# A decoder layer on one core: FFN2's norm takes its second columns by squares and an exchange, with three blocks summed meanwhile

## The chip, the cores and the metric

The kernel runs on one core of one Trainium2 chip. The metric is the device time of the whole program in microseconds, the median of several runs. A core has a matrix engine (TensorE, here PE), three engines for elementwise work (VectorE: DVE, ScalarE: ACT, GpSimd: POOL) and a queue engine, SyncE (SP), which issues most of the transfers between main memory and the on-chip memory. Matmul results land in PSUM, eight banks of 128 rows by 512 float32 columns.

## The reference

One layer on 256 tokens of 1024 columns, all float32. Both feed-forward parts (FFN1 and FFN2) have 2816 hidden columns.

```python
h = x
h = h + 0.5 * swiglu(rms_norm(h, ffn1_norm), ffn1_w_gate, ffn1_w_up, ffn1_w_down)
h = h + hybrid_mixer(rms_norm(h, mix_norm), ...)      # projection, two attentions, gates, W_out
h = h + 0.5 * swiglu(rms_norm(h, ffn2_norm), ffn2_w_gate, ffn2_w_up, ffn2_w_down)
out = rms_norm(h, final_norm)

swiglu(x, g, u, d) = (silu(x @ g) * (x @ u)) @ d
rms_norm(x, g) = x * rsqrt(mean(x * x) + 1e-6) * g
```

## The kernel before

The 256 tokens are two halves of 128, t = 0 and t = 1. Every weight matrix is cut into tiles of 128 x 512, which lie in main memory as one stream `wstream`, in the order of use; a DMA on SP fetches a chunk of two tiles (512 KB) into a buffer `raw`. The first 12 chunks have buffers of their own, all later ones share three, so that a chunk's DMA starts when DVE has read the second tile of the chunk three before it. Each tile is split into a high part `wh` by ACT (L163 and L160) and the rest `wl` by DVE (L164 and L161), in ten buffers each. Activations are split likewise (`zh` and `zl` for the norm "z" ahead of FFN2). A product is three matmuls, wh with the high activations, wl with the high ones, and wh with the low ones (`mm3`, L292 to L294). These three are called a unit here. A split buffer comes free when t = 1 has used its tile.

FFN1 and FFN2 each run through 11 blocks of 256 hidden columns. A block is eight tiles k = 0 to 7 (128 rows of the model dimension each, gate and up side by side) for each t, and its sums fill one PSUM bank for each t. `hidden(b, t)` then evacuates a bank: ACT takes the silu of its first 256 columns (L432), DVE multiplies it with the other 256 (L433) and transposes the product in blocks of 32 x 32 (L441). Within a block t = 1 lags t = 0 by some units (`lagged`): by 2 from block 1 on, by 8 in FFN2's block 0. FFN1's block 0 goes by pairs (`unit_pair`).

PSUM comes in three kinds: `acc_bank` (one bank, 3 buffers), `y_bank` (one, 1 buffer) and `two_banks` (one tile of two banks, 2 buffers). FFN1's block 0 takes one two-bank tile for both t, later blocks take `acc_bank`.

The order of PE and SP is written by hand; the other engines' order is too, except in stretches where a scheduler places their instructions. `Weave` lets side work advance by a step with each unit (`tick`), after a delay given in units (the constants `D_...`). `W.pump` splits weight tiles ahead.

A norm's activations need the tokens' rows transposed (`Normed`). The first 512 columns (c = 0) go by `moved`: DVE transposes squares of 32 x 32, 16 DMAs exchange the squares, and ACT and DVE split the result. The second 512 columns (c = 1) go by `half`: four PE transposes (`tp_z`, 128 x 128 each) into PSUM, then the split. The factor 1/rms (`inv_rms`) is applied in `hidden`. At the start x comes in transposed from the host already (`xt`), and x itself (`h`, two loads of 512 KB) is needed only for the squares of the norm and for the residual.

Of the kernel before, what the change touches and what calls it, by code (L numbers as in the profile page):

```python
# [8 lines left out]
F32 = mybir.dt.float32  # L9
# [12 lines left out]
KD = D // P  # L22
# [22 lines left out]
D_NORM = 4  # L45
D_SQUARES = 3
D_EIGHT = 6
D_MERGE = 8
D_FIRST = (9, 10)
D_RMS0 = 4  # L50
D_RMS1 = 5
AHEAD0 = 4
N_WARM = 10
D_LANE = 11
# [134 lines left out]
def hybrid_layer_kernel(ctx, tc, x, xt, pos, g_final, bgate, wstream, out):  # L189
    nc = tc.nc  # L190
# [18 lines left out]
    def big(nm, dt=F32R):  # L209
        return work.tile([P, 1024], dt, name=nm, tag="big", bufs=24)  # L210
# [16 lines left out]
    def gain(i):  # L227
        for n, (lo, hi) in enumerate(((0, FB * KD), (W_IN, W_BR), (W_FFN2, W_FFN2 + FB * KD))):
            if lo <= i < hi:
                k = n * KD + (i - lo) % KD  # L230
                return gk[:, k:k + 1]
        return None

    W = Weights(nc, wpool, lambda nm: big(nm, F32), wstream, gain, WB, AHEAD0)
# [17 lines left out]
    load_x(nc.sync, 6, 8)  # L252
    W.load(4)
    nc.sync.dma_start(h[0], x[0:P, :])
    W.load(5)
    nc.sync.dma_start(h[1], x[P:T, :])
    W.load(6)
    nc.sync.dma_start(posi, pos)


# [35 lines left out]
    def unit(o, a, w, first, last):  # L296
        mm3(o, a[0], a[1], w, first, last)
        weave.tick()
        W.pump()
# [12 lines left out]
    def split(dst_h, dst_l, src, hi_engine=None, rest=nc.vector):  # L312
        (hi_engine or nc.scalar.copy)(dst_h, src)
        rest.tensor_sub(dst_l, src, dst_h.bitcast(F32))
# [26 lines left out]
    class Normed:  # L341
# [15 lines left out]
        def moved(self, c):  # L357
# [7 lines left out]
            split(plain(self.parts[0][:, s]), plain(self.parts[1][:, s]), slots(q[:, 512:1024], 4))  # L365
            self.there.add(c)

        def rms(self):
            weave.begin(inv_rms(self.t, self.nm, self.r))

# [4 lines left out]
    class Given(Normed):  # L375
# [15 lines left out]
        def blk(self, k):  # L391
            o = k % 4 * T + self.t * P
            return [q[:, o:o + P] for q in self.made[k // 4 * 2:k // 4 * 2 + 2]]

    def lagged(n, lag):

        for k in range(n + lag):
            if k < n:
                yield 0, k
            if k >= lag:  # L400
                yield 1, k - lag
# [4 lines left out]
    def slots(q, n):  # L406

        return q[:, 0:n * P].rearrange("p (g s w) -> p s g w", g=4, s=n)

    def plain(q):  # L410
        return q.rearrange("p (s g w) -> p s g w", g=4, w=32)

    def exchange(moved, squares, n, queues, gap):

        w = 32
        for m in range(16):
            i, j = divmod(m, 4)
            queues[m % len(queues)].dma_start(moved[j * w:j * w + w, i * n * w:(i + 1) * n * w],
                                              squares[i * w:i * w + w, j * n * w:(j + 1) * n * w])
            if m % len(queues) == len(queues) - 1:  # L420
                yield gap


    def ffn(base, xn, nm, on_half, lag, last=False):


        hts = {}
        squares = {}

        def hidden(b, t, bank):  # L430
            sh = wide(f"sh_{nm}{b}_{t}", 512)
            silu = nc.scalar.activation(sh[:, 0:256], bank[:, 0:256], AF.Silu, scale=xn[t].r)  # L432
            prod = nc.vector.scalar_tensor_tensor(sh[:, 256:512], bank[:, 256:512], xn[t].r, sh[:, 0:256],  # L433
                                                  op0=ALU.mult, op1=ALU.mult)
            marks["silu"], marks["prod"] = silu.ins, prod.ins
            p = b // 2
            n = min(8, 4 * (FB - 2 * p))
            if p not in squares:
                squares[p] = big(f"hs_{nm}{b}", F32)
            dst = slots(squares[p], n)[:, b % 2 * 4 + t:b % 2 * 4 + t + 3:2]  # L440
            nc.vector.transpose(dst, plain(sh[:, 256:512]))  # L441
            if t == 1 and (b % 2 or b == FB - 1):
                weave.add(turn_hidden(p, n), D_TURNED)

        def later(f, *args):
            f(*args)
            return
            yield

        def turn_hidden(p, n):  # L450
            moved = big(f"hm_{nm}{p}", F32)
            yield from exchange(moved, squares[p], n, [nc.sync], D_MOVE)
            yield D_MOVED
            hts[p] = big(f"hth_{nm}{p}"), big(f"htl_{nm}{p}")
            split(plain(hts[p][0][:, 0:n * P]), plain(hts[p][1][:, 0:n * P]), slots(moved, n))

        for b in range(FB):
            if b == 1:
                W.ahead = AHEAD
            if b == 1 and last:  # L460
                ordered.enter_context(tc.manual_schedule())
            banks = {}
            if b == 0 and lag == 0:
                pair = two_banks(f"gu_{nm}0")
                banks = {t: pair[:, t * 512:t * 512 + 512] for t in range(2)}
                for k in range(KD):
                    unit_pair([banks[t] for t in range(2)], [xn[t].blk(k) for t in range(2)], W.get(base + k),
                              k == 0, k == KD - 1)
                    W.done(base + k)
                for t in range(2):  # L470
                    weave.add(later(hidden, b, t, banks[t]), D_FIRST[t])
            for t, k in lagged(KD, 2 if b else lag) if b or lag else ():
                if k == 0:
                    banks[t] = acc_bank(f"gu_{nm}{b}_{t}")
                i = base + b * KD + k
                unit(banks[t], xn[t].blk(k), W.get(i), k == 0, k == KD - 1)
                if t == 1:
                    W.done(i)
                if k == KD - 1:
                    weave.add(later(hidden, b, t, banks[t]), 0 if b else D_FIRST[t])  # L480

        base += FB * KD
        banks = {}

        def out_bank(t, c):
            if (t, c) not in banks:
                if (t, c) != (1, 1):
                    banks[t, c] = acc_bank(f"dn_{nm}{t}{c}")
                else:
                    banks[t, c] = y_bank(f"dn_{nm}{t}{c}")  # L490
            return banks[t, c]

        def down(t, c, k, i, piece=None):

            o = k % 4 * 256 + t * P
            ht = [q[:, o:o + P] for q in hts[k // 4]]
            w = W.get(i)
            if piece is not None:
                if k == head:
                    banks[piece] = two_banks(f"dn_{nm}p{piece}")  # L500
                cols = slice(piece * 256, piece * 256 + 256)
                mm3(banks[piece][:, 0:256], *ht, [q[:, cols] for q in w], k == head, k == KF - 1)
                weave.tick()
                W.pump()
            else:
                unit(out_bank(t, c), ht, w, k == 0, k == (head - 1 if last and (t, c) == (1, 1) else KF - 1))

        def residual(t, c, piece=None):
            if piece is None:
                ps, s = banks[t, c][:, 0:512], slice(c * 512, c * 512 + 512)  # L510
            else:
                ps = banks[piece][:, 0:256]
                s = slice(c * 512 + piece * 256, c * 512 + piece * 256 + 256)
            nc.vector.scalar_tensor_tensor(h[t][:, s], ps, 0.5, h[t][:, s], op0=ALU.mult, op1=ALU.add)

        tail = TAILS[2 if last else 1]
        head = KF - tail
        for k in range(head):
            for c in range(2):
                for t in range(2):  # L520
                    down(t, c, k, base + 2 * k + c)
                W.done(base + 2 * k + c)
        if not last:
            ordered.close()
        weave.flush()
        if last:

            residual(1, 1)
        for t, c in ((0, 0), (0, 1), (1, 0), (1, 1)) if last else ((0, 0), (1, 0), (0, 1), (1, 1)):
            pieces = (0, 1) if last and (t, c) == (1, 1) else (None,)  # L530
            for piece in pieces:
                for k in range(head, KF):
                    i = base + 2 * head + c * tail + k - head
                    down(t, c, k, i, piece)
                    if t == 1 and piece in (None, 1):
                        W.done(i)
                residual(t, c, piece)
                on_half(t, c, piece)
# [84 lines left out]
    un = [None, None]  # L623

    def next_norm(dst, nm):
        def on_half(t, c, piece=None):
            def go():
                dst[t].half(c)
                dst[t].rms()
                return  # L630
                yield

            if c == 0:
                dst[t] = Normed(t, nm)
                weave.begin(dst[t].moved(c))
            else:
                weave.add(go(), D_NORM)

        return on_half
# [415 lines left out]
```

## Time and profile before

| what | value |
|---|---|
| median of 3 runs | 556.6 us (556.47 to 556.66) |
| the profiled execution | 555.9 us, its span 554.2 us |
| busy PE | 546.1 us (99%) |
| busy DVE, ACT, POOL | 401.3 us (72%), 338.1 us (61%), 70.1 us (13%) |
| mean granted TensorE clock | 0.997 |
| read from main memory | 102.25 MB |

The span goes from the first to the last instruction. What the time holds beyond it (555.9 - 554.2 = 1.7 us) is not in the trace. Busy shares are means over all stages. Where PE is named with a wait, nothing else hid it. One matmul's own duration is printed as 0.39 us, but matmuls are pipelined: the distance from one to the next is what counts.

### The profile page before, as it was taken

The numbers are of one execution on the slowest core, as the hardware profiler recorded it, in microseconds if no ns is written. First come the engines' busy times: TensorE is split into PE (matmuls) and PEld (weight loads), VectorE is DVE, ScalarE is ACT, GpSimd is POOL, SyncE is SP. The second block draws the span as 40 slices with busy tenths as digits, with TensorE's granted clock in tenths as the row PEclk, the third lists the DMA queues.
The fourth block names the chain that finished last, engine by engine and source line by source line (L and its number), as shares of the span: only waits on it lengthen the run. The fifth ranks groups of instructions, "written<-read, shape, count | busy, mean of one in ns | idle before, by whom it ended". The sixth has DMA issues, their size and how long they took to land.

```text
span 554.2 us, 7853 instructions
## 1 busy us (share of the span) xinstructions
PE 546.1 (99%) x2494; PEld 449.5 (81%) x2494; DVE 401.3 (72%) x694; ACT 338.1 (61%) x576; POOL 70.1 (13%) x141
## 2 busy tenths in 40 slices
PE   9999999999999999999999999999999999999995
PEld 5788888888888888888888888888888888888884
DVE  6887788766466676889888888777677678655645
ACT  6865656655454767677875774476556566544633
POOL 1200000000003746022022200460000000000000
PEclk9999999999999999999999999999999999999998
DMA  8946766775685677455545464576657766757722
GB/s 311 403 141 202 220 216 216 220 237 184 210 235 179 200 232 220 155 159 183 176 151 172 137 202 149 179 242 216 219 180 234 238 206 200 229 179 230 243 79 76
DMA packets 42937, 111.69 MB, mean 202 GB/s; under 512 B 8080, under 2 KB 16528, under 8 KB 42896
## 3 DMA queue, kind: packets, MB, share of 16 engines
q1 hardware_dynamic: 40464, 107.90, 60.9%
q0 software_dynamic: 2000, 2.62, 1.8%
q10 hardware_dynamic: 432, 0.67, 0.3%
q8 instruction: 19, 0.31, 0.3%
q14 instruction: 22, 0.18, 0.1%
HBM read 102.25 MB, written 1.05 MB: 186 GB/s over the span
## 4 chain that ended last, share of the span: by engine, by line
PE 95%; DMA 3%; ACT 0%; DVE 0%; issue 0%; ACTq 0%
PE gu_f L293 14%; PE gu_f L294 14%; PE gu_f L292 14%; PE dn_f L294 7%; PE dn_f L292 7%; PE dn_f L293 7%; PE in L292 7%; PE in L294 7%; PE in L293 7%; DMA raw<-in_wstream 2%; PE wo L294 1%; PE wo L292 1%; PE wo L293 1%; PE y_a L748 1%; PE z L748 1%; PE y_b L748 1%
## 5 line engine op out<-in xcount | busy, mean ns | idle before, releaser
L164 DVE SCALAR_TENSOR_TENSOR wl<-raw,first,wh 128x512 fp32r<-128x512 f32 x256 | 181.8, 747 | 41.3 <-ACT wh L163 40.1
L163 ACT ACTIVATE wh<-raw,first 128x512 fp32r<-128x512 f32 x256 | 171.7, 717 | 56.3 <-DMA raw<-in_wstream 31.0
L160 ACT CAST wh<-raw 128x512 fp32r<-128x512 f32 x120 | 70.4, 620 | 63.9 <-DMA raw<-in_wstream 40.8
L161 DVE TENSOR_TENSOR wl<-raw,wh 128x512 fp32r<-128x512 f32 x120 | 78.6, 691 | 40.0 <-ACT wh L160 39.9
L292 PE MATMUL gu_f<-wh,zh 128*128 128x512 f32 x176 | 68.6, 390 | 0.0
L294 PE MATMUL gu_f<-wh,zl 128*128 128x512 f32 x176 | 68.5, 389 | 0.0
L293 PE MATMUL gu_f<-wl,zh 128*128 128x512 f32 x176 | 68.5, 389 | 0.0
L292 PE MATMUL dn_f<-wh,hth_f 128*128 128x512 f32 x172 | 67.1, 390 | 0.0
L294 PE MATMUL dn_f<-wh,htl_f 128*128 128x512 f32 x172 | 66.9, 389 | 0.0
L293 PE MATMUL dn_f<-wl,hth_f 128*128 128x512 f32 x172 | 66.9, 389 | 0.0
L292 PE MATMUL in<-wh,uh 128*128 128x512 f32 x160 | 63.5, 397 | 0.0
L293 PE MATMUL gu_f<-wl,xh 128*128 128x512 f32 x160 | 62.4, 390 | 0.3 <-DVE wl L164 0.3
L294 PE MATMUL in<-wh,ul 128*128 128x512 f32 x160 | 62.5, 391 | 0.0
L292 PE MATMUL gu_f<-wh,xh 128*128 128x512 f32 x160 | 62.4, 390 | 0.1
L293 PE MATMUL in<-wl,uh 128*128 128x512 f32 x160 | 62.4, 390 | 0.0
L294 PE MATMUL gu_f<-wh,xl 128*128 128x512 f32 x160 | 62.2, 389 | 0.0
L293 PEld LDWEIGHTS gu_f<-wl,zh 128*128 128x128 f32 x176 | 33.0, 188 | 6.9
L294 PEld LDWEIGHTS gu_f<-wh,zl 128*128 128x128 f32 x176 | 33.0, 188 | 6.8
L292 PEld LDWEIGHTS gu_f<-wh,zh 128*128 128x128 f32 x176 | 33.0, 188 | 6.8
L292 PEld LDWEIGHTS dn_f<-wh,hth_f 128*128 128x128 f32 x172 | 32.3, 188 | 6.9 <-DVE sh_f L433 0.4
L294 PEld LDWEIGHTS dn_f<-wh,htl_f 128*128 128x128 f32 x172 | 32.3, 188 | 6.7
L293 PEld LDWEIGHTS dn_f<-wl,hth_f 128*128 128x128 f32 x172 | 32.3, 188 | 6.7
(247 smaller groups left out, 756.5 us busy)
## 6 DMA issues: line engine op xcount, KB each, us to landing
raw<-in_wstream SPq DMA_DIRECT2D x184, 512.0 KB, 4.3
hm_f<-hs_f SPq DMA_DIRECT2D x160, 32.0 KB, 4.2
raw<-in_wstream SPq DMA_DIRECT2D x8, 256.0 KB, 4.9
h<-in_x SPq DMA_DIRECT2D x2, 512.0 KB, 6.6
bg<-in_bgate POOLq DMA_DIRECT2D x4, 256.0 KB, 4.6
xin<-in_xt SPq DMA_DIRECT2D x3, 256.0 KB, 5.1
hm_f<-hs_f SPq DMA_DIRECT2D x32, 16.0 KB, 3.1
gB<-in_g_final POOLq DMA_DIRECT2D x1, 512.0 KB, 6.2
```

The costliest lines, as they stand in the source:

```text
L160: self.nc.scalar.copy(hi, raw)
L161: self.nc.vector.tensor_sub(lo, raw, hi.bitcast(F32))
L163: self.nc.scalar.activation(hi, raw, AF.Copy, scale=g)
L164: self.nc.vector.scalar_tensor_tensor(lo, raw, g, hi.bitcast(F32), op0=ALU.mult, op1=ALU.subtract)
L292: nc.tensor.matmul(o, ah, wh, start=first, stop=False)
L293: nc.tensor.matmul(o, ah, wl, start=False, stop=False)
L294: nc.tensor.matmul(o, al, wh, start=False, stop=last)
L748: nc.tensor.matmul(o, a[p], b[q], start=first and i == 0, stop=last and i == 2, skip_group_check=True)
```

## The change

Three things are moved.

At the start, the DMA of the second half of x is issued after weight chunk 5 (tiles 10 and 11) and no longer before it. The square of that half (`D_RMS1`) and FFN1's `hidden(0, 1)` (`D_GIVEN`) come later by some units.

In the norm ahead of FFN2, the second columns of both t no longer take PE's transposes. `moved_both` transposes squares on DVE for t = 0 and then t = 1, exchanges both together by 16 DMAs of 32 KB on SP and POOL, and splits the result.

So that FFN2 can begin without the second columns, `three_blocks` sums the blocks 0, 1 and 2 on the first columns first (24 units with a lag of 8), and then on the second columns (24 units with a lag of 2). The weight stream's order on the host follows, and so does `gain`. Six sums are open meanwhile: blocks 0 and 1 of one t take the two halves of one two-bank tile (`gu_f2 01`), block 2 takes an `acc_bank`. The order is written by hand from block 3 on, where it was from block 1 on.

```diff
-D_FIRST = (9, 10)
+D_GIVEN = (9, 15)
-D_RMS1 = 5
+D_RMS1 = 9
...
     nc.sync.dma_start(h[0], x[0:P, :])
-    W.load(5)
+    W.load(6)
     nc.sync.dma_start(h[1], x[P:T, :])
-    W.load(6)
     nc.sync.dma_start(posi, pos)
...
+        @staticmethod
+        def moved_both(c, norms):
+
+            s = slice(c * 512, c * 512 + 512)
+            squares, moved = [big(f"{norms[0].nm}{i}{c}", F32) for i in "sm"]
+            for t in range(2):
+                nc.vector.transpose(slots(squares, 8)[:, t:t + 7:2], plain(h[t][:, s]))
+                yield None if t == 0 else D_SQUARES
+            yield from exchange(moved, squares, 8, [nc.sync, nc.gpsimd], 1)
+            yield D_BOTH
+            for t in range(2):
+                split(plain(norms[t].parts[0][:, s]), plain(norms[t].parts[1][:, s]), slots(moved, 8)[:, t:t + 7:2])
+                norms[t].there.add(c)
+                yield 1
...
+    def three_blocks(x, base, banks, evac):
+
+        for c in range(2):
+            for t, n in lagged(12, 2 if c else KD):
+                b, k = divmod(n, 4)
+                i = base + c * 12 + n
+                unit(banks(t, b), x[t].blk(c * 4 + k), W.get(i), c == 0 and k == 0, c == 1 and k == 3)
+                if t == 1:
+                    W.done(i)
+                if c == 1 and k == 3:
+                    evac(b, t, banks(t, b))
...
-            if b == 1 and last:
+            if b == 3 and last:
                 ordered.enter_context(tc.manual_schedule())
...
+            if b == 0 and lag:
+                gus = {}
+
+                def gu_bank(t, b):
+                    if (t, b) not in gus:
+                        if b == 0:
+                            pair = two_banks(f"gu_{nm}01{t}")
+                            gus[t, 0], gus[t, 1] = pair[:, 0:512], pair[:, 512:1024]
+                        else:
+                            gus[t, b] = acc_bank(f"gu_{nm}{b}_{t}")
+                    return gus[t, b]
+
+                three_blocks(xn, base, gu_bank, lambda b, t, ps: weave.add(later(hidden, b, t, ps)))
+            for t, k in lagged(KD, 2) if b > (2 if lag else 0) else ():
...
+            elif nm == "z":
+                weave.add(later(dst[t].rms), D_NORM)
+                if t == 0:
+                    both.append(Normed.moved_both(c, dst))
+                    next(both[0])
+                else:
+                    weave.begin(both[0])
...
+        if n == 2:
+            res = [res[b * KD + c * 4 + k] for c in range(2) for b in range(3) for k in range(4)] + res[3 * KD:]
```

Three places show how instructions move. The first is PE in FFN2, where block 0 ends and the next sum goes on. `wh251` is the high part of tile 251; `gu_f20_0` is block 0 of t = 0 and `gu_f20_1` block 0 of t = 1. Before, block 0 of t = 1 ends and block 1 begins in another bank, waiting for its weights alone (`waits DVE` on a row with a `wl` is for that part):

```order
L292 MATMUL gu_f20_1_4035<-wh251_3982,zh1_3829 128x512
L293 MATMUL gu_f20_1_4035<-wl251_3983,zh1_3829 128x512
L294 MATMUL gu_f20_1_4035<-wh251_3982,zl1_3830 128x512
L292 MATMUL gu_f21_0_4082<-wh252_3991,zh0_3766 128x512 [waits Activation_49]
L293 MATMUL gu_f21_0_4082<-wl252_3992,zh0_3766 128x512 [waits DVE_49]
L294 MATMUL gu_f21_0_4082<-wh252_3991,zl0_3767 128x512
```

In the change, `gu_f2010` is the two-bank tile of blocks 0 and 1 for t = 0, and `gu_f2011` that for t = 1. The tiles 256 to 259 are block 0 on the second columns, and 260 is block 1's first tile there:

```order
L294 MATMUL gu_f2010_3966<-wh259_4102,zh0_3766 128x512
L295 MATMUL gu_f2010_3966<-wl259_4103,zh0_3766 128x512
L296 MATMUL gu_f2010_3966<-wh259_4102,zl0_3767 128x512
L294 MATMUL gu_f2011_4043<-wh257_4084,zh1_3829 128x512
L295 MATMUL gu_f2011_4043<-wl257_4085,zh1_3829 128x512
L296 MATMUL gu_f2011_4043<-wh257_4084,zl1_3830 128x512
L294 MATMUL gu_f2010_3966<-wh260_4113,zh0_3766 128x512 [waits DVE_49]
L295 MATMUL gu_f2010_3966<-wl260_4114,zh0_3766 128x512
L296 MATMUL gu_f2010_3966<-wh260_4113,zl0_3767 128x512
```

Block 0 of t = 0 is complete with tile 259, one unit of t = 1 follows, and then tile 260 adds to block 1 of t = 0 in the same two-bank tile, with a wait for DVE. Counted out, that wait is for the product of `hidden(0, 0)`, which is the last reader of block 0's half. Five units on, tile 260 for t = 1 waits in the same way for the product of `hidden(0, 1)`.

The second place is ACT around the first silu of FFN2 (`sh_f20_0`), ahead of which the table of functions is loaded. Before:

```order
L163 ACTIVATE wh252_3991<-raw126_3920,first_73 128x512 [waits DMAHW2_49]
L163 ACTIVATE wh253_4008<-raw126_3920,first_73 128x512
L432 ACT_TABLE_LOAD [waits PE_49]
L432 ACTIVATE sh_f20_0_4086<-gu_f20_0_3969,r_z0_3768 128x256 [waits Pool_49]
L163 ACTIVATE wh254_4042<-raw127_3946,first_73 128x512 [waits DMAHW3_49,PE_49]
```

In the change:

```order
L315 CAST zh0_3766<-zm1_3897 128x512 [waits DMAHW0_49,DMASW7_49,DMAHW1_49,DMASW6_49,DMAHW2_49,DMASW5_49,DMAHW3_49,DMASW4_49,DMAHW4_49,DMASW3_49,DMAHW5_49,DMASW2_49,DMAHW6_49,DMASW1_49,DMASW0_49]
L315 CAST zh1_3829<-zm1_3897 128x512
L164 ACTIVATE wh260_4113<-raw130_4066,first_73 128x512 [waits DMAHW6_49,DVE_49,PE_49]
L164 ACTIVATE wh261_4121<-raw130_4066,first_73 128x512 [waits DVE_49,PE_49]
L164 ACTIVATE wh262_4139<-raw131_4088,first_73 128x512 [waits DMAHW7_49,DVE_49,PE_49]
L164 ACTIVATE wh263_4146<-raw131_4088,first_73 128x512 [waits DVE_49,PE_49]
L164 ACTIVATE wh264_4155<-raw132_4106,first_73 128x512 [waits DMAHW0_49,DVE_49,PE_49]
L164 ACTIVATE wh265_4165<-raw132_4106,first_73 128x512 [waits DVE_49,PE_49]
L164 ACTIVATE wh266_4182<-raw133_4125,first_73 128x512 [waits DMAHW1_49,PE_49]
L466 ACT_TABLE_LOAD [waits PE_49]
L466 ACTIVATE sh_f20_0_4174<-gu_f2010_3966,r_z0_3768 128x256 [waits Pool_49]
L164 ACTIVATE wh267_4192<-raw133_4125,first_73 128x512 [waits DVE_49,PE_49]
```

The table's load and the silu stood behind tile 253, they now stand behind tile 266, whose chunk (`raw133`) takes the buffer that tile 261 (`raw130`) leaves. The two casts of the second columns (`zm`) stand right behind tile 259 and ahead of tile 260. DVE has the same order, with the product of `hidden(0, 0)` right behind `wl266`.

The third place is DVE in FFN1, from the split of tile 17 on (`raw_265` of the change and `raw_271` of before hold tiles 16 and 17). Before:

```order
L164 SCALAR_TENSOR_TENSOR wl_323<-raw_271,first,wh_322 128x512 [waits PE_49,Activation_49]
L164 SCALAR_TENSOR_TENSOR wl_332<-raw_291,first,wh_331 128x512 [waits DMAHW5_49,Activation_49]
L433 SCALAR_TENSOR_TENSOR sh_f_0_338<-gu_f_156,r_x_124,sh_f_0_338 128x256 [waits Activation_49]
L441 STREAM_TRANSPOSE hs_f_341<-sh_f_0_338 128x2x4x32 [waits DVE_49]
L164 SCALAR_TENSOR_TENSOR wl_344<-raw_291,first,wh_343 128x512 [waits Activation_49]
L433 SCALAR_TENSOR_TENSOR sh_f_1_352<-gu_f_156,r_x_125,sh_f_1_352 128x256 [waits Activation_49]
L441 STREAM_TRANSPOSE hs_f_341<-sh_f_1_352 128x2x4x32 [waits DVE_49]
L164 SCALAR_TENSOR_TENSOR wl_360<-raw_310,first,wh_359 128x512 [waits DMAHW6_49,Activation_49]
L164 SCALAR_TENSOR_TENSOR wl_370<-raw_310,first,wh_369 128x512 [waits Activation_49]
L433 SCALAR_TENSOR_TENSOR sh_f_0_378<-gu_f_0_260,r_x_124,sh_f_0_378 128x256 [waits Activation_49]
```

In the change:

```order
L165 SCALAR_TENSOR_TENSOR wl_321<-raw_265,first,wh_320 128x512 [waits PE_49,Activation_49]
L340 TENSOR_SCALAR v_x_277<-r_x_125,v_x_277 128x1 [waits DVE_49]
L341 TENSOR_SCALAR r_x_125<-v_x_277,r_x_125 128x1 [waits DVE_49]
L165 SCALAR_TENSOR_TENSOR wl_332<-raw_284,first,wh_331 128x512 [waits DMAHW5_49,Activation_49]
L467 SCALAR_TENSOR_TENSOR sh_f_0_338<-gu_f_156,r_x_124,sh_f_0_338 128x256 [waits Activation_49]
L475 STREAM_TRANSPOSE hs_f_341<-sh_f_0_338 128x2x4x32 [waits DVE_49]
L165 SCALAR_TENSOR_TENSOR wl_344<-raw_284,first,wh_343 128x512 [waits Activation_49]
L165 SCALAR_TENSOR_TENSOR wl_356<-raw_304,first,wh_355 128x512 [waits DMAHW6_49,Activation_49]
L165 SCALAR_TENSOR_TENSOR wl_366<-raw_304,first,wh_365 128x512 [waits Activation_49]
L467 SCALAR_TENSOR_TENSOR sh_f_0_374<-gu_f_0_257,r_x_124,sh_f_0_374 128x256 [waits Activation_49]
L475 STREAM_TRANSPOSE hs_f_341<-sh_f_0_374 128x2x4x32 [waits DVE_49]
L467 SCALAR_TENSOR_TENSOR sh_f_1_381<-gu_f_156,r_x_125,sh_f_1_381 128x256 [waits Activation_49]
```

The last steps of the second half's 1/rms (`v_x`, `r_x`) stood between the splits of tiles 11 and 14 and now stand between those of tiles 15 and 18, and the product of block 1 (`gu_f_0_257`, before `gu_f_0_260`) now comes ahead of that of block 0 of t = 1. On PE, block 2 of t = 1 waits for that product of block 1 in both kernels, because its bank is the one that block 1 of t = 0 had.

## Rows read from the trace of the kernel before

**Rows 1.** The page: busy time, and the chain that ended last, by engine

```profile
PE 546.1 (99%) x2494; PEld 449.5 (81%) x2494; DVE 401.3 (72%) x694; ACT 338.1 (61%) x576; POOL 70.1 (13%) x141
PE 95%; DMA 3%; ACT 0%; DVE 0%; issue 0%; ACTq 0%
```

**Rows 2.** The chain at the start: start us, us, what

```profile
9.33 7.82 DMA raw<-in_wstream
18.01 0.76 DVE wl L164
```

**Rows 3.** Timeline of PE, FFN1: start, us, engine, line, operation [idle, releaser]

```profile
17.04 0.39 PE L292 MATMUL gu_f<-wh,xh 128*128 128x512 f32 x1
...
18.03 0.49 PE L292 MATMUL gu_f<-wh,xh 128*128 128x512 f32 x1
18.82 0.50 PE L293 MATMUL gu_f<-wl,xh 128*128 128x512 f32 x1 [0.29 <-DVE wl L164]
19.15 0.39 PE L294 MATMUL gu_f<-wh,xl 128*128 128x512 f32 x1
```

**Rows 4.** Timeline of ACT at the start

```profile
15.94 1.06 ACT L319 ACTIVATE sq_v_x<-h 128x1024 bf16<-128x1024 f32 x1
...
17.25 3.35 ACT L163 ACTIVATE wh<-raw,first 128x512 fp32r<-128x512 f32 x5 [0.17 <-DMA raw<-in_wstream]
```

**Rows 5.** Timeline of DVE at the start

```profile
21.18 0.74 DVE L164 SCALAR_TENSOR_TENSOR wl<-raw,first,wh 128x512 fp32r<-128x512 f32 x1
...
22.28 3.40 DVE L164 SCALAR_TENSOR_TENSOR wl<-raw,first,wh 128x512 fp32r<-128x512 f32 x5
25.59 0.48 DVE L433 SCALAR_TENSOR_TENSOR sh_f<-gu_f,r_x,sh_f 128x256 f32<-128x256 f32 x1
...
26.48 0.71 DVE L164 SCALAR_TENSOR_TENSOR wl<-raw,first,wh 128x512 fp32r<-128x512 f32 x1
```

**Rows 6.** Second half of x: issue on SP; KB, us to landing

```profile
8.70 0.33 SPq L256 DMA_DIRECT2D h<-in_x  x1
...
h<-in_x SPq DMA_DIRECT2D x1, 512.0 KB, 7.2
```

**Rows 7.** The chain around the start of FFN2, longest pieces

```profile
364.21 0.44 PE tp_z L353 x4
```

**Rows 8.** Timeline of PE, FFN2's first block and second block

```profile
367.23 0.39 PE L292 MATMUL gu_f<-wh,zh 128*128 128x512 f32 x1
...
371.07 0.40 PE L292 MATMUL gu_f<-wh,zh 128*128 128x512 f32 x1
...
390.13 0.39 PE L292 MATMUL gu_f<-wh,zh 128*128 128x512 f32 x1
```

**Rows 9.** Timelines of PE and ACT in FFN1, a buffer set free and taken

```profile
42.98 0.39 PE L294 MATMUL gu_f<-wh,xl 128*128 128x512 f32 x1
...
43.41 0.73 ACT L163 ACTIVATE wh<-raw,first 128x512 fp32r<-128x512 f32 x1 [0.49 <-PE gu_f L294]
```

**Rows 10.** Timeline of DVE: low part of a piece of the norm

```profile
370.84 0.69 DVE L314 TENSOR_TENSOR zl<-zq,zh 128x512 fp32r<-128x512 f32 x1 [0.61 <-ACT zh L313]
```

**Rows 11.** Timelines of ACT and DVE, FFN2's first evacuation

```profile
373.38 1.28 ACT L432 ACT_TABLE_LOAD   x1 [0.97 <-PE gu_f L294]
374.67 0.47 ACT L432 ACTIVATE sh_f<-gu_f,r_z 128x256 f32<-128x256 f32 x1
...
375.18 0.48 DVE L433 SCALAR_TENSOR_TENSOR sh_f<-gu_f,r_z,sh_f 128x256 f32<-128x256 f32 x1 [1.73 <-ACT sh_f L432]
```

**Rows 12.** Chunks issued 373 to 389, then one: KB, us to landing

```profile
raw<-in_wstream SPq DMA_DIRECT2D x7, 512.0 KB, 3.3
...
raw<-in_wstream SPq DMA_DIRECT2D x1, 512.0 KB, 4.8
```

**Rows 13.** Windows: busy PE, PEld, DVE, ACT, POOL; PEclk, DMA, GB/s

```profile
550.00:551.00 1.00, 0.00 (x0) 0.00 (x0) 0.29 (x1) 0.52 (x1) 0.00 (x0) 1.00 0.00 0
551.00:552.00 1.00, 0.00 (x0) 0.00 (x0) 0.00 (x0) 0.00 (x0) 0.00 (x0) 0.50 0.86 318
```

More of the change, by code (lines that the diff above doesn't have):

```diff
@@ L47 @@
 D_EIGHT = 6
+D_BOTH = 8
 D_MERGE = 8
-D_FIRST = (9, 10)
+D_GIVEN = (9, 15)
 D_RMS0 = 4
-D_RMS1 = 5
+D_RMS1 = 9
 AHEAD0 = 4
@@ L229, in gain @@
             if lo <= i < hi:
-                k = n * KD + (i - lo) % KD
-                return gk[:, k:k + 1]
+                k = (i - lo) % KD
+                if n == 2 and i - lo < 3 * KD:
+                    k = (i - lo) // 12 * 4 + (i - lo) % 4
+                return gk[:, n * KD + k:n * KD + k + 1]
         return None
@@ L393, in blk, with later @@
             return [q[:, o:o + P] for q in self.made[k // 4 * 2:k // 4 * 2 + 2]]
+    def later(f, *args):
+        f(*args)
+        return
+        yield
     def lagged(n, lag):
@@ L443, in hidden @@
                 weave.add(turn_hidden(p, n), D_TURNED)
[L445 to L448, printed above, removed]
         def turn_hidden(p, n):
@@ L470, in ffn @@
                 for t in range(2):
-                    weave.add(later(hidden, b, t, banks[t]), D_FIRST[t])
-            for t, k in lagged(KD, 2 if b else lag) if b or lag else ():
+                    weave.add(later(hidden, b, t, banks[t]), D_GIVEN[t])
+            if b == 0 and lag:
[10 more added lines that the diff above has]
+            for t, k in lagged(KD, 2) if b > (2 if lag else 0) else ():
                 if k == 0:
@@ L479, in ffn @@
                 if k == KD - 1:
-                    weave.add(later(hidden, b, t, banks[t]), 0 if b else D_FIRST[t])
+                    weave.add(later(hidden, b, t, banks[t]))
         base += FB * KD
@@ L625, in next_norm @@
     def next_norm(dst, nm):
+        both = []
         def on_half(t, c, piece=None):
```

## The prediction

> **What bounds the kernel.** I read the page first. PE is busy for 99% of the span, and the chain that ended last is PE for 95% and DMA for 3% [rows 1]. So work moved among ACT, DVE, POOL and the queues counts only where it makes PE wait, and a change gains only what it takes off PE's own stream or out of PE's few waits. Hence I looked for those waits, and for the distance from unit to unit. In FFN2 the 28 units from 371.07 to 390.13 take 0.681 us each [rows 8], so one matmul counts 0.227.
>
> **The start, removed.** In FFN1's block 1, PE runs tile 9 at 17.04; tile 10 should follow at 17.72 and its third matmul at 18.17, but that one starts at 19.15 [rows 3]. The loss is 0.98. The chain gives the reason: chunk 5 was issued at 9.33 and took 7.82 [rows 2], then ACT's `wh` ran at 17.25 [rows 4] and DVE's `wl` at 18.01 [rows 2]. With the new order chunk 5 takes the place of x's second half, issued at 8.70 and landing 7.2 later, at 15.9 [rows 6]. ACT is free for tile 10 at 15.94, where the square stood [rows 4], so its `wl` starts before 17.3 and PE, which wants it at 17.95, does not wait. The 0.98 goes.
>
> **The start, added.** The square (17.25 - 15.94 = 1.31 on ACT [rows 4]) now follows tile 12. Tile 12 was the third of five splits that ran gapless from 17.25 at 0.67 apart [rows 4], so its chunk had landed by 18.59. Tile 12 ends at about 19.26, the square at 20.57, `wh` 13 follows, and 0.76 behind it (18.01 - 17.25) `wl` 13 at 21.33. Before, it started at 21.18 [rows 5], so little is late up to here. But DVE still has three steps of 1/rms to interleave, which stretch a split from 0.66 to 1.10 (22.28 - 21.18) [rows 5]. From 21.33: tile 14 at 22.00, tiles 15 to 18 at about 1.10 apart, the last at 26.4, the product of `hidden(0, 0)` at 27.1 where it was 25.59 [rows 5], the next split 0.89 later (26.48 - 25.59), two more at 0.66, and the product of block 1 at about 29.9, done at 30.4. PE's block 2 for t = 1 waits for that. It stands 19 units into block 1's stream, which began one unit before 17.04, thus at 16.36 + 12.94 = 29.30 without any loss, and 30.28 with before's loss. The new wait is as long as the old one, within what this sum can tell: **net 0**. If chunk 6 lands earlier, some of the 0.98 remains as a gain; if each step is a little later, 0.3 is lost. Range of this term: -0.98 to +0.3.
>
> **FFN2, removed.** Two groups of four PE transposes, each 0.44 in the chain [rows 7]: **-0.88**. The squares on DVE, the 16 DMAs and the second columns' casts take their place on engines with slack. Are they in time? PE needs the second columns 24 units after its start at 367.23 - 0.44 = 366.79 (the first group is gone), at 383.1. The casts stand in ACT behind tile 259. That tile takes the split buffer of tile 249, set free by unit 17 for t = 1. ACT followed such a release 0.43 behind the start of the last matmul (42.98 to 43.41) [rows 9], so `wh259` starts at 366.79 + 0.28 (next part) + 11.58 + 0.45 + 0.43 = 379.53, and the casts end near 381.4. That leaves 1.7 us; below I take this cover as given, and late transfers would add what exceeds it.
>
> **FFN2, tile 10.** With a lag of 8 and ten buffers, the eleventh tile of the stage waits for t = 1's first unit. Release to `wh` 0.43, `wh` to `wl` 0.76, `wl` to matmul 0.81 (18.82 - 18.01) make 2.00; PE's order leaves eight matmuls, 1.82. It loses 0.18 and about 0.10 for filling again (19.15 - 18.82 is 0.33, not 0.23) [rows 3]: **+0.28**, or nothing if a link is shorter.
>
> **FFN2, the new wait.** Unit 30 (t = 0, tile 260) waits for the product of `hidden(0, 0)`, because blocks 0 and 1 share a two-bank tile. Without a wait it would start at 366.79 + 0.28 + 20.43 = 387.50. Block 0 is complete with unit 28, whose last matmul starts at 386.59, so only one unit lies between. Two chains lead to that product.
> The shorter one: ACT reacts 0.43 later, loads the table (374.67 - 373.38 = 1.29), runs the silu, DVE's product starts 0.51 behind it (375.18) and takes 0.48 [rows 11], and PE starts about 0.06 on (18.82 against 18.01 + 0.75). It gives 386.59 + 2.77 = 389.36: a wait of 1.86, the least possible.
> The longer one: the table's load stands in ACT behind `wh266`. Its chunk takes the raw buffer that `wl261` leaves. DVE starts `wl259` at 380.29 and goes on with two low parts of the second columns (0.69 each [rows 10]), `wl260` and `wl261`, five in all at some 0.67 apart, done at 383.7. The chunk lands 3.3 later by the median of this stretch, 4.8 at most [rows 12], at 387.0 to 388.5. Then 0.10 to ACT's start, 0.67 for `wh266`, and 1.29 + 0.51 + 0.48 + 0.06: PE goes on between 390.1 and 391.6. The wait is 2.6 to 4.1. I take the median's, as the queue has no exchange of `hm` running here, with the refill: **+2.7**. In before's trace the same load of the table was free, since nobody waited for its bank.
>
> **The load, by row and by rule.** The row shows 1.29 from the load's start to the silu, but ACT had idled 0.97 before it [rows 11]. The Trainium skill (*ScalarE: Activation LUTs*, What ACT_TABLE_LOAD costs) gives about 1283 ns and a drain of about 1380 ns on top. By the row the sum stays, by the page it would be 1.4 larger.
>
> **FFN2, the second wait.** Unit 35 (t = 1, tile 260) waits for the product of `hidden(0, 1)`. Block 0 of t = 1 ends with unit 33. From the start of its last matmul 0.43 + 0.51 + 0.48 + 0.06 = 1.48, against four matmuls, 0.91: 0.57 and the refill, **+0.67**. No table is loaded any more, and tiles 267 and 268 stand before this silu with their buffers free by then. Blocks 1 and 2 are evacuated with more room, and from block 3 on the stream is as before.
>
> **The sum.** 0 - 0.88 + 0.28 + 2.7 + 0.67 = +2.8. On the profiled execution's 555.9 that is 558.7. It stood 0.7 below the median of the runs, 556.6, so the forecast is 559.4.
>
> **The rivals.**
> *No wait at unit 30, faster.* The halves of the tile are different banks; were the wait only nominal, PE would go on at once, leaving -0.88 + 0.28, at best also the start's -0.98: 555.0 to 556.0. It decides if the product is done by 387.4. The Trainium skill (*Perfetto Trace Analysis*, Matmuls) says that independent groups in different banks let evacuation overlap the next matmuls; that is what this rival would be. Against it stands the row of the new order: tile 260's matmul waits for DVE, and with 1.86 as the least price the wait alone outweighs both gains. For this rival the count of the wait, or the distance of two units, must be wrong.
> *The short chain decides.* Chunk 133 lands before 386.5, for instance because its buffer came free earlier. The wait falls to 1.86 + 0.10, the time to 558.6. If the start's gain remained too, 557.7.
> *The load costs more behind busy ACT.* Up to the 0.97 that idle time could have hidden: 560.4.
> *The clock falls.* PE idles 2.7 us. With PE idle from 550 to 551 the granted clock was 1.00, and in the next microsecond 0.50 [rows 13], the lower level, 1.2 GHz. Should it fall here, each microsecond at that level costs 0.5; three of them would give 560.9. For it: PE idles nowhere that long before. Against it: a whole idle microsecond at 1.00.
>
> **Chances.** The forecast, long chain at its length between 2.6 and 4.1: 0.58 (558.9 to 560.9). The short chain: 0.14. The costlier load: 0.08. The clock: 0.08. No wait: 0.12. A measurement of this kernel tells about 0.2%, 1.1 us, from no change. The last rival lies near that line: of its 0.12 I count 0.08 faster and 0.04 as the same; another 0.03 for the same are short chains with the start's gain whole and tile 10 free. Slower: 0.85. The range, 556.8 to 561.0, leaves out most of the last rival and the clock's worse half.
>
> **What would show it.** Right, if the profile after has PE without a gap at 17.7 to 19, a gap of about 1 at 29.3; no `tp_z`; one gap of 2.6 to 4.1 near 387.5 with DVE's product as releaser, ACT's `wh266` waiting for a DMA ahead of it, and one of 0.6 five units later. The forecast is wrong if PE shows no gap in FFN2 (the dependency was misread), if the gap ends on the casts of the second columns instead (their exchange is late), or if it is longer and the clock row shows 0.50.

## The result and the profile after

The changed kernel takes 562.72 us in the median of 4 runs (562.02 to 563.22), the kernel before 556.54 (4 runs). The ratio is 1.0113, with a 95% interval of 1.0101 to 1.0125. It is slower, as forecast, but by 6.2 us where 2.8 were forecast, and outside the range. Of the runs below, one of experiment 11 and two of before in its session were disturbed; they are left out of the ratios.

The profiled execution took 562.02, its span is 560.0 (554.2 before). First the page of the kernel after, the lines that answer to [rows 1], and the granted clock in 40 slices of the span:

```profile
span 560.0 us, 7873 instructions
PE 547.9 (98%) x2486; PEld 449.9 (80%) x2486; DVE 403.3 (72%) x696; ACT 339.6 (61%) x576; POOL 72.5 (13%) x149
...
PEclk9999999999999999999999999999899999999998
...
PE 91%; DMA 4%; DVE 2%; ACT 1%; issue 1%; SPq 0%; DVEq 0%; ACTq 0%
```

PE's share of the chain fell from 95% to 91%, and DVE, ACT and DMA took what it lost. In the clock's row there is one digit below 9 between the ends, two thirds through the span. That slice is FFN2's beginning. PE's waits say the same (line, waited for: us in total, times, longest):

```profile
PE gu_f L294 <- DVE sh_f L467: 4.5, 3, 3.5
PE warm L285 <- DVE zeros L264: 1.1, 1, 1.1
```

Three waits of 4.5 us in all end on DVE's products, where before there was none. The timeline of PE at the start, for [rows 3]:

```profile
16.67 0.39 PE L294 MATMUL gu_f<-wh,xh 128*128 128x512 f32 x1
...
18.10 0.39 PE L294 MATMUL gu_f<-wh,xh 128*128 128x512 f32 x1
18.33 0.40 PE L295 MATMUL gu_f<-wl,xh 128*128 128x512 f32 x1
18.56 0.39 PE L296 MATMUL gu_f<-wh,xl 128*128 128x512 f32 x1
...
29.47 0.39 PE L296 MATMUL gu_f<-wh,xl 128*128 128x512 f32 x1
30.42 0.50 PE L294 MATMUL gu_f<-wh,xh 128*128 128x512 f32 x1 [0.57 <-DVE sh_f L467]
```

Tile 10's three matmuls, at 18.10 to 18.56, follow at 0.23 each: the gap of 0.98 is gone. A gap has come at 30.42, behind the product of block 1 (`sh_f`, 0.57 of it listed as PE's wait). Next the timeline of ACT in FFN2, from the casts of the second columns on, for [rows 11]:

```profile
380.50 1.12 ACT L315 CAST zh<-zm 128x512 fp32r<-128x512 f32 x2
381.53 1.33 ACT L164 ACTIVATE wh<-raw,first 128x512 fp32r<-128x512 f32 x2
383.57 1.34 ACT L164 ACTIVATE wh<-raw,first 128x512 fp32r<-128x512 f32 x2 [0.70 <-DMA raw<-in_wstream]
386.56 1.34 ACT L164 ACTIVATE wh<-raw,first 128x512 fp32r<-128x512 f32 x2 [1.65 <-DMA raw<-in_wstream]
388.33 0.72 ACT L164 ACTIVATE wh<-raw,first 128x512 fp32r<-128x512 f32 x1 [0.43 <-DMA raw<-in_wstream]
389.06 1.28 ACT L466 ACT_TABLE_LOAD   x1
390.36 0.47 ACT L466 ACTIVATE sh_f<-gu_f,r_z 128x256 f32<-128x256 f32 x1
```

The two casts come at 380.50, close behind tile 259 and without waiting for the exchange. Tiles 260 to 265 follow, with waits for their chunks; tiles 264 and 265 wait 1.65 for theirs and are done at 387.90. Tile 266 comes at 388.33, behind a DMA: its chunk was issued at 384.05 and took 4.2. Only then do the table's load (389.06) and the silu (390.36) follow. PE meanwhile:

```profile
387.55 0.39 PE L296 MATMUL gu_f<-wh,zl 128*128 128x512 f32 x1
391.41 0.50 PE L294 MATMUL gu_f<-wh,zh 128*128 128x512 f32 x1 [3.47 <-DVE sh_f L467]
391.75 0.49 PE L295 MATMUL gu_f<-wl,zh 128*128 128x512 f32 x1
392.04 0.63 PE L296 MATMUL gu_f<-wh,zl 128*128 128x512 f32 x1
392.47 0.63 PE L294 MATMUL gu_f<-wh,zh 128*128 128x512 f32 x1
...
394.60 0.63 PE L296 MATMUL gu_f<-wh,zl 128*128 128x512 f32 x1
395.03 0.53 PE L294 MATMUL gu_f<-wh,zh 128*128 128x512 f32 x1
395.40 0.39 PE L295 MATMUL gu_f<-wl,zh 128*128 128x512 f32 x1
...
397.17 0.50 PE L294 MATMUL gu_f<-wh,zh 128*128 128x512 f32 x1 [0.45 <-DVE sh_f L467]
```

The last matmul before the wait starts at 387.55. The next should follow at 387.77 and comes at 391.41, 3.64 later. But behind it the distance from matmul to matmul is 0.43 and no longer 0.23, until 395.03. The second wait, at 397.17, is 0.6 long. The windows show what the slow matmuls are (the window's length; busy share of PE, PEld, DVE, ACT and POOL, with their instructions; PEclk, DMA share and GB/s):

```profile
387.00:388.00 1.00, 0.94 (x5) 0.43 (x3) 0.68 (x2) 0.90 (x2) 0.00 (x0) 1.00 0.77 217
...
390.00:391.00 1.00, 0.00 (x0) 0.00 (x0) 0.13 (x1) 0.99 (x3) 0.00 (x0) 1.00 0.88 270
391.00:392.00 1.00, 0.59 (x2) 0.48 (x3) 0.97 (x3) 0.44 (x1) 0.00 (x0) 0.95 0.47 180
392.00:393.00 1.00, 1.00 (x4) 0.77 (x3) 0.46 (x1) 0.00 (x0) 0.00 (x0) 0.50 0.06 25
...
394.00:395.00 1.00, 1.00 (x3) 0.74 (x3) 0.26 (x1) 0.71 (x1) 0.00 (x0) 0.50 1.00 393
395.00:396.00 1.00, 1.00 (x5) 0.84 (x4) 0.49 (x1) 0.00 (x0) 0.00 (x0) 0.84 0.10 37
396.00:397.00 1.00, 0.72 (x4) 0.24 (x2) 0.37 (x1) 0.88 (x2) 0.00 (x0) 1.00 0.00 0
```

PE idled through 388 to 391 at a granted clock of 1.00. It began again in the window from 391, and from 392 to 395 the clock was 0.50, the lower of the two levels (1.2 GHz), while PE was busy all the time.

### The profile page after: what moved, and what is told of

It reads as the page before. It is cut to its first block, busy times and chain, and to the rows that moved or that the text cites. A ratio compares the mean times of both kernels' runs of the same rounds, so it can differ in the third digit from the quotient of the medians.

```text
span 560.0 us, 7873 instructions
## 1 busy us (share of the span) xinstructions
PE 547.9 (98%) x2486; PEld 449.9 (80%) x2486; DVE 403.3 (72%) x696; ACT 339.6 (61%) x576; POOL 72.5 (13%) x149
## 4 chain that ended last, share of the span: by engine, by line
PE 91%; DMA 4%; DVE 2%; ACT 1%; issue 1%; SPq 0%; DVEq 0%; ACTq 0%
PE gu_f L294 12%; PE gu_f L295 12%; PE gu_f L296 12%; PE dn_f L296 7%; PE dn_f L295 7%; PE dn_f L294 7%; PE in L294 7%; PE in L296 7%; PE in L295 7%; DMA raw<-in_wstream 2%; DVE wl L165 2%; PE wo L294 1%; PE wo L296 1%; PE wo L295 1%; DMA xin<-in_xt 1%; PE y_a L800 1%
```

## The experiments

The times of before differ a little from session to session, so each ratio is to the runs of before of its own session: 556.36 us for the first four experiments, 556.47 for the next four, 556.38 for the last.

**1. The start alone,** on the kernel before: the three constants and the order of the DMAs.

```diff
-D_FIRST = (9, 10)
+D_FIRST = (9, 15)
-D_RMS1 = 5
+D_RMS1 = 9
...
-    W.load(5)
+    W.load(6)
     nc.sync.dma_start(h[1], x[P:T, :])
-    W.load(6)
```

> The kernel before with the new order of the start alone. Theory (the start is a swap of one wait for another, and the loss lies in FFN2): the wait at tile 10 (0.98) is gone, block 2 of t = 1 waits 0.6 to 0.9 for the product of block 1, and the time is that of before within 0.3, 556.2 to 556.9. Rival (the start makes a good part of the loss, since the whole of FFN1 runs later): 558 or more.

556.18 us (11 runs), ratio 0.9994 (0.9985 to 1.0003). One wait went and another came: in its profile PE waits 0.47 for the product of block 1. The start alone costs nothing: its interval includes 1.

**2. Blocks 0 and 2 share the tile.** One line of the change differs, the one that hands out the halves:

```diff
-                            gus[t, 0], gus[t, 1] = pair[:, 0:512], pair[:, 512:1024]
+                            gus[t, 0], gus[t, 2] = pair[:, 0:512], pair[:, 512:1024]
```

> The changed kernel, but the two-bank tile of one t holds blocks 0 and 2, and block 1 has a bank of its own. Between block 0's end and the next matmul into its tile there are then ten units and no longer two. Theory (the shared tile makes the waits, and the wait makes the clock fall): both waits go (3.7 and 0.7 with the refill) and so does the time at the lower clock (1.6), 556.4 to 557.0. Rival (the exchange on the queues or the late split of the second columns makes it slower): 561 or more.

555.88 us (10 runs), ratio 0.9992 (0.9983 to 1.0001). In its profile the load and the silu are as late as in the change (389.13 and 390.43), the exchange and ACT's order are the same:

```profile
389.13 1.28 ACT L466 ACT_TABLE_LOAD   x1
390.43 0.48 ACT L466 ACTIVATE sh_f<-gu_f,r_z 128x256 f32<-128x256 f32 x1
```

PE has no wait for a product in FFN2 (only the two small gaps at tile 10 there, 0.28 in all), and no window from 386 to 399 is below 1.00. All of the loss, 6.2 us and a little more, hung on which two blocks share a tile.

**3. Matmuls in the gap,** 15 into the idle y bank, read by nobody, ahead of the matmul that waits:

```diff
+                if c == 1 and t == 0 and n == 4:
+                    idle = y_bank("idle")
+                    for _ in range(15):
+                        nc.tensor.matmul(idle, x[0].blk(0)[0], W.get(i)[0], start=True, stop=True)
```

> The changed kernel with 15 extra matmuls into the unused y bank ahead of the matmul that waits (3.4 us of work whose result nobody reads). The wait ends when it did before. Theory (the granted clock falls because PE idles there): the clock stays at 1.00 after the wait and the 1.6 us come back, 560.8 to 561.4. Rival (the lower clock has another cause, or the slow matmuls after the wait are no matter of the clock): 562.4 to 563.0, with rows at 0.50 as before.

560.63 us, ratio 1.0075 (1.0062 to 1.0089), 2.1 less than the change. The timeline of PE, and the windows behind the wait:

```profile
387.91 3.56 PE L455 MATMUL idle<-wh,zh 128*128 128x512 f32 x15
391.67 0.50 PE L295 MATMUL gu_f<-wh,zh 128*128 128x512 f32 x1 [0.19 <-DVE sh_f L472]
```

```profile
391.00:392.00 1.00, 0.81 (x4) 0.35 (x3) 0.84 (x2) 0.70 (x2) 0.00 (x0) 1.00 0.52 213
392.00:393.00 1.00, 1.00 (x6) 0.82 (x5) 0.73 (x2) 0.00 (x0) 0.00 (x0) 1.00 0.04 16
393.00:394.00 1.00, 1.00 (x6) 0.84 (x5) 0.00 (x0) 0.64 (x1) 0.00 (x0) 1.00 0.44 61
```

The block's next matmul starts at 391.67, no earlier than in the change, so the end of the wait is untouched. The clock stays at 1.00, though the wait is as long as in the change. So PE's idling made the slow stretch.

**4. The transposes back,** the three blocks kept (the branch `elif nm == "z"` of `next_norm` taken out).

> The changed kernel with three blocks summed as in the change, but the second columns of the norm by PE transposes as before, without the exchange. Theory (the shared tile decides): the wait stays, about 1.3 shorter since DVE has not the two low parts ahead of tile 261, so 2.3, with 0.9 for the transposes back, and the clock falls or not: 559.5 to 562.5. Rival (the exchange is what costs): 556.6 to 557.2, no wait over 0.5 in FFN2.

562.86 us, ratio 1.0122 (1.0106 to 1.0137). The exchange is not what costs. But the wait is 3.4 and not 2.3. The whole stretch lies 1.1 later here (unit 30 was due at 388.90, in the change at 387.77). Tile 261's chunk landed at 382.5, where ACT waits 0.8 for it, and DVE had split the tile at 384.7, which is 4.2 ahead of unit 30; with the low parts in the change it was 3.8. So the two low parts cost 0.4 there and not 1.3, and 0.1 of the wait. What is left is the chain of the three raw buffers (a chunk lands, is split, and only then does the chunk three on start), which experiment 7 tries.

**5. The table loaded earlier,** behind the last square of the norm.

```diff
         square(t, m, slice(0, D))
+        if nm == "z" and t == 1:
+            with tc.issue_after(marks["sq"]):
+                nc.scalar.preload_act_table_set("silu_and_others")
```

> The changed kernel with the table of silu loaded right behind the last square of FFN2's norm, 20 us before it is needed. Theory (the load lies on the chain that PE waits for): the wait is 1.29 shorter, 2.2 to 2.5 in place of 3.6. If the clock holds over such an idle time, 2.9 less than the change: 559.4 to 560.2. If it falls all the same: 561.0 to 561.8. Rival (the load costs nothing there, another link sets the end): the wait stays at 3.5 and the time at that of the change, 562.4 to 563.

561.84 us, ratio 1.0098 (1.0083 to 1.0113), and the wait is 3.1. This run does not tell the two apart, as the edit moved more than the load. The scheduler put POOL's eight DMAs of the exchange behind all steps of 1/rms: the first at 374.26, the last near 378, where the change has four from 370.09 and the last at 374.92. ACT's timeline in this run:

```profile
382.70 1.14 ACT L315 CAST zh<-zm 128x512 fp32r<-128x512 f32 x2 [1.74 <-DMA raw<-in_wstream]
...
389.48 0.72 ACT L164 ACTIVATE wh<-raw,first 128x512 fp32r<-128x512 f32 x1 [1.81 <-DMA raw<-in_wstream]
390.10 0.45 ACT L469 ACTIVATE sh_f<-gu_f,r_z 128x256 f32<-128x256 f32 x1
```

The casts come 2.2 us later than in the change, and tile 266 1.15 later. That ate most of the 1.29. (The row names the weight chunk as what ended ACT's wait at 382.70; the exchange's last DMA, issued at 377.8, took 4.6 and landed just ahead of it.) It is a side result: the exchange has little slack, since in the change it lands at 378.8 for casts at 380.50, and two microseconds more of it reach PE.

**6. The order as written from FFN2's first block on** (`if b == 0 and last`), so that the silu stands ahead of tile 266.

> The changed kernel with ACT's and DVE's order taken as written from FFN2's first block on, not from block 3 on. The table's load and the first silu then stand ahead of tile 266 and so need no chunk 133. Theory (the place behind tile 266 lengthens the wait): the load starts when tile 265 is split, at 387.9, and the wait is 2.3 to 2.6: 559.5 to 560.3 with the clock up, 561.1 to 561.9 with it down. Rival (the place in ACT does not matter): 562.4 to 563, wait 3.5.

562.35 us (559.61 to 562.80), ratio 1.0094 (1.0074 to 1.0114), wait 3.7. Time and wait are close to the rival's (562.4 and 3.5), but this does not show that the place in ACT is of no account, for the reason of experiment 5: in this order too, half of POOL's DMAs came behind 1/rms (from 377.44 on), the casts waited for the exchange until 382.81, and tiles 264 and 265 came at 388.12. The place ahead of tile 266 was bought with a later tile 265.

**7. Four raw buffers** in place of three.

```diff
-... tag="raw", bufs=3)
+... tag="raw", bufs=4)
...
-            self.load(i // CH + 1 + 3)
+            self.load(i // CH + 1 + 4)
```

> The changed kernel with four raw buffers in place of three; the order of ACT stays, with the load and the silu behind tile 266. Chunk 133 then takes the buffer that tile 259 leaves and is issued near 381.5. Theory (the ring of raw buffers makes tile 266 late): the short chain is left, block 0's end, the table, silu and product, a wait of 1.8 to 2.0: 559.0 to 559.8 with the clock up. Rival (the wait is long for another reason, the order or the exchange): 562 or more.

559.01 us (558.15 to 559.70), ratio 1.0043 (1.0030 to 1.0057). ACT's timeline in the profiled run, and PE's matmul that waited:

```profile
386.22 0.73 ACT L164 ACTIVATE wh<-raw,first 128x512 fp32r<-128x512 f32 x1 [1.06 <-PE gu_f L296]
386.96 1.28 ACT L466 ACT_TABLE_LOAD   x1
388.26 0.47 ACT L466 ACTIVATE sh_f<-gu_f,r_z 128x256 f32<-128x256 f32 x1
```

```profile
389.31 0.50 PE L294 MATMUL gu_f<-wh,zh 128*128 128x512 f32 x1 [1.76 <-DVE sh_f L467]
```

Tile 266 waits for its split buffer now (PE), not for a chunk, and comes two microseconds earlier. The wait is 1.8, the bound that was worked out for the short chain. What I had not expected: the clock fell here too, behind 1.8 us of idling (0.60 in the window from 390, 0.50 from 391 to 393):

```profile
391.00:392.00 1.00, 1.00 (x4) 0.81 (x3) 0.00 (x0) 0.44 (x1) 0.00 (x0) 0.50 0.50 135
```

The profiled run, 559.70, is the longest of the four, with a mean clock of 0.993; the other three, 558.15 to 559.02, have 0.996 to 0.998.

**8. A faster version:** the halves as in experiment 2, a lag of 7 in place of 8, and FFN1's first evacuations behind block 1's (`D_GIVEN = (16, 17)`).

```diff
-            for t, n in lagged(12, 2 if c else KD):
+            for t, n in lagged(12, 2 if c else KD - 1):
...
-D_GIVEN = (9, 15)
+D_GIVEN = (16, 17)
```

> The changed kernel with three edits: blocks 0 and 2 share the two-bank tile, the lag of the first 24 units is 7 in place of 8, and at the start both evacuations of FFN1's block 0 come after the first one of block 1. Theory: without the two waits of FFN2 that is 555.9 by the earlier run; the lag takes the wait at tile 10 of FFN2 (0.3), the order at the start takes block 2's wait for the product (0.5): 554.9 to 555.5, faster than before by 0.15 to 0.3%. Rival (these waits come back at the next link, as DVE at the start is late for other tiles): 555.7 to 556.3.

554.80 us (6 runs), ratio 0.9971 (0.9959 to 0.9982): faster than both kernels. PE's list of waits in its profile is one line, the warm-up at the program's beginning:

```profile
PE warm L285 <- DVE zeros L264: 1.0, 1, 1.0
```

**9. The table behind the last cast** of the first columns, which leaves POOL's and SP's order as in the change.

> The changed kernel with silu's table loaded behind the last cast of the norm's first columns; unlike the run that loaded it behind the square, POOL's and SP's order stay as in the change, so the exchange is not later. Theory (the load is a link of 1.29 in the chain that ends the wait): a wait of 2.2 to 2.5. The clock fell behind shorter waits too, so 561.0 to 561.8; 559.4 to 560.2 if it holds. Rival (the load is no link, and the earlier run's time says so): wait 3 or more, 562 or more.

561.28 us (558.73 to 561.73), ratio 1.0077 (1.0059 to 1.0094). ACT's timeline:

```profile
388.66 0.72 ACT L164 ACTIVATE wh<-raw,first 128x512 fp32r<-128x512 f32 x1 [1.31 <-DMA raw<-in_wstream]
389.29 0.45 ACT L469 ACTIVATE sh_f<-gu_f,r_z 128x256 f32<-128x256 f32 x1
```

Tile 266 is no earlier than in the change, the silu follows 0.63 behind it and not 2.03. The wait is 2.5. The load was a link of the chain, with its whole length. In the profiled run the clock fell again:

```profile
392.00:393.00 1.00, 1.00 (x4) 0.81 (x3) 0.00 (x0) 0.03 (x1) 0.00 (x0) 0.50 0.56 180
```

One of the four runs, at a mean clock of 0.997, took 558.73, the profiled one, at 0.993, 561.20.

**10. Both,** the table of experiment 9 and four raw buffers.

> The change with both: the table loaded early, and four raw buffers. Only the shortest chain is left, the end of block 0, silu, product: 1.48 against the 0.9 that the order leaves. Theory: a wait of 0.5 to 0.8 at block 1's second columns, the second wait of 0.6 as before, and the granted clock stays at 1.00 as PE hardly idles: 557.0 to 558.2. Rival (the clock falls for another reason than the idle time, such as the silu or the load of the queues): rows at 0.50 here too, 558.8 or more.

557.41 us (10 runs), ratio 1.0020 (1.0011 to 1.0028). PE's waits:

```profile
PE gu_f L294 <- DVE sh_f L470: 1.6, 3, 0.6
PE warm L285 <- DVE zeros L264: 1.1, 1, 1.1
PE gu_f L307 <- DVE xl L316: 0.3, 1, 0.3
```

The longest in FFN2 is 0.6, no window from 387 to 397 is below 1.00, and all ten runs lie between 557.29 and 557.90. Behind at most 0.6 us of idling the clock did not fall.

**11 and 12. The faster version without its edit at the start,** with `D_GIVEN = (9, 15)` as in the change, and **with the whole start of the kernel before.**

> The fast version without its edit at the start: blocks 0 and 2 share the tile, lag 7, and the start of the change as it is. Theory: block 2's wait for the product in FFN1 is back, 0.5 to 0.6 and the refill: 555.3 to 555.7. Rival (that wait is made up for later): 554.6 to 555.0, as the fast version.

> The fast version with the start of the kernel before (second half of x ahead of chunk 5, its square and FFN1's first evacuations where they were). Theory: the wait at tile 10 of FFN1, 1.0 with its refill, is back and replaces nothing: 555.5 to 556.0. Rival (the start's order is worth nothing in either form): 554.6 to 555.1.

555.45 us (11 runs), ratio 0.9982 (0.9973 to 0.9991), and 555.96 us (11 runs), ratio 0.9991 (0.9983 to 1.0000). Against the ratio of experiment 8 the start's order is worth 0.6 and 1.1 us, each about as much as the wait that comes back: 0.7 with its refill for block 2 in the one, 0.9 at tile 10 in the other. So loading x's second half later does gain its microsecond, if the evacuations move too. Experiment 11 differs from experiment 2 by the lag alone, and the gaps at tile 10 of FFN2 are gone in it.

## Why the prediction was right in kind and wrong in size

**The mechanism held.** Every step that the prediction named is in the profile: no gap at tile 10 and a new one behind block 1's product (forecast to start at 29.9, and at 29.89 in the trace), no `tp_z`, a wait at tile 260 for the product of `hidden(0, 0)`, `wh266` waiting for a DMA ahead of the load, a second wait five units on. Experiment 2 shows that the shared tile makes the waits, since it changes nothing else. One of the prediction's own signs of being wrong is there too: the clock's row at 0.50.

**The terms,** by the two profiled executions (spans 554.2 and 560.0, 5.8 apart):

| term | forecast | measured |
|---|---|---|
| start | 0 | +0.2 (unit 0 of FFN2 at 367.03 for 366.79; FFN1's block 1 had begun 0.3 later, at 16.67), alone -0.2 by the medians of experiment 1 |
| transposes | -0.88 | -0.88 (two groups of [rows 7]; by their absence, as the trace after has none) |
| tile 10 of FFN2 | +0.28 | +0.31 (unit 30 was due at 387.77, 20.74 behind unit 0 at 367.03; 30 units are 20.43) |
| wait at unit 30 | +2.7 | +3.64 and 0.1 refill |
| lower clock | 0 | +1.6 (units 30 to 34 took 391.41 to 396.55 where 3.4 and the refill were due) |
| wait at unit 35 | +0.67 | +0.6 and 0.1 refill |

They add up to 5.7.

They show two steps that failed.

**Failed: the clock, put at nothing in the sum.** The prediction made it a rival of 0.08 and argued against it with "a whole idle microsecond at 1.00" from [rows 13]. That row was misread. PE's last matmul in the kernel before ends at 547.6, so ahead of that microsecond lie 2.4 more of idling at 1.00:

```profile
547.00:548.00 1.00, 0.58 (x5) 0.37 (x4) 0.92 (x4) 0.21 (x2) 0.00 (x0) 1.00 0.57 207
548.00:549.00 1.00, 0.00 (x0) 0.00 (x0) 0.72 (x4) 0.81 (x3) 0.00 (x0) 1.00 0.00 0
```

The clock fell at 551 all the same. These rows show a fall that trails PE's stop, and so 1.00 during an idle stretch is no sign against one. In the change the clock was at 1.00 through the whole wait as well, and it fell within a microsecond of PE's beginning again. The price in that rival, half a microsecond for each microsecond at the lower level and three of them, was right (1.6). With it the forecast would have been 561.0. Experiments 3 and 10 show the cause from two sides, the gap filled and the gap shortened.

**Mis-sized: the wait at unit 30, by the chunks' landing.** The wait was put at the lower end of its own range, with the stretch's median of 3.3 for chunk 133 [rows 12]; it took 4.2, and the wait was 1.0 longer, within the 2.6 to 4.1 that were given. Not all of this is due to chunk 133. Chunk 132, issued at 381.41, took 5.0, so ACT was done with tile 265 only at 387.90, and tile 266 started 0.43 behind that; the prediction had no tiles 264 and 265 in its chain. Why the two were late stays open. In experiments 2, 3, 4 and 9 chunk 133 was issued with chunk 132 still under way for 1.7 to 2.1 us (2.4 in the change) and took 4.2 to 4.5; in experiment 5 chunk 132 had 0.3 to go, and chunk 133 took 3.4. But in the kernel before a chunk issued 1.5 ahead of another's landing took 3.1, and no experiment was made for this. Experiment 7 shows the rest of that step right: without the raw buffer's delay the wait is the 1.8 of the short chain.

The rivals were priced one at a time, each beside a wait at its lower end. The measured wait and the measured clock together give 562.0, outside the range, which ended at 561.0.

**What the rivals did.** The one on the other side, no wait, failed at once. That the load costs more than its row failed too: from load to silu it is 1.30 (389.06 to 390.36), directly behind a busy ACT, and experiment 9 took 1.40 out of the distance from tile 266 to the silu. The Trainium skill (*ScalarE: Activation LUTs*, What ACT_TABLE_LOAD costs) adds a drain of about 1380 ns to the load, about 2.66 us in all; neither number here has room for it.

**What stays open.** How much the fall of the clock costs in the runs that have no profile: 1.6 by the slow matmuls of the profile, 2.1 by the median of experiment 3, 2.5 between two runs of experiment 9. The spread within experiments 6, 7 and 9 fits a fall that comes in some executions and not in others, but a run's mean clock alone does not show where it fell. Whether the matmul into the other half of the tile needed to wait at all was not tried; the runs show only that it did, and what pairing other blocks gives. Whether four raw buffers help the faster version was not tried either.

## What to carry to other kernels

When sums are paired into one PSUM tile that the scheduler guards as a whole, pair the one that is evacuated with the one that is written last, and count the units from the first's end to the other's next write: two were too few here, ten were plenty. Price a wait of PE with what follows it: behind the waits of 1.8 to 3.7 us here the matmuls ran at half clock in the profiled runs, and a profile in which PE never idles can show the like only at its end. And check what a small edit does to the order on every engine, as two experiments here (5 and 6) were undone by POOL's DMAs moving behind arithmetic.

## What was unexpected of the hardware

In the change the granted clock did not fall while PE idled (1.00 from 388 to 391), but just after it had begun again, and stayed at 0.50 for three windows of 1 us although PE was busy throughout; it was back at 1.00 by 396. At the end of the kernel before it fell with PE still idle, at 551 behind a stop at 547.6. So it came behind PE's stop in both, once with PE at work again and once without. The idling ahead of it was 3.6 us in the change, 2.5 in experiment 9 and 1.8 in experiment 7; after 0.6 (experiment 10) no window was below 1.00. The beginning of the program also varies: FFN1's block 1 began between 16.2 and 17.1 in the profiled runs, though PE's work ahead of it is the same in all, so a few tenths between two profiled executions need not be the edit's.
